# A hybrid decoder layer on one core: the values of the linear-attention branch stored as one array, and full copies moved behind both high halves

## The chip, the core and the metric

The kernel runs on one core of one Trainium2 chip. What counts is the device time of one execution in microseconds, as a median of several runs. Beside the times there is a profile of one execution. In it PE is TensorE's matmuls, PEld its weight loads, DVE VectorE, ACT ScalarE, POOL GpSimd, and SP the engine that here issues the DMAs (SPq in the rows is SP's queue of them).

## The reference

Input x has 1024 tokens of width 1024, all in float32. The layer normalizes x, projects it once with the wide matrix w_in, and feeds two token mixers: a gated linear attention (GLA, 4 heads, keys of 128, values of 256, a decay for each key channel) and a stick-breaking attention (8 heads of 128). Cut to what matters here:

```python
h = rmsnorm(x, norm_g)
proj = h @ w_in
(g_q, g_k, g_v, g_gate, g_rank,
 s_q, s_k, s_v, s_gate, m_logits) = jnp.split(proj, SPLIT_IDX, axis=-1)
log_a = jax.nn.log_sigmoid((g_rank @ w_dec_up + b_dec).astype(jnp.float32)) / GLA_TAU
o_gla = gla_chunked(g_q, g_k, g_v, log_a)      # o_t = q_t S_t, S_t = diag(alpha_t) S_{t-1} + k_t v_t
o_gla = rmsnorm(o_gla, gla_norm_g) * jax.nn.silu(g_gate)
o_sb = stick_breaking(s_q, s_k, s_v) * jax.nn.silu(s_gate)
gates = jax.nn.sigmoid(m_logits + b_gate)
merged = gates[:, :, 0] * (o_gla @ w_pa) + gates[:, :, 1] * (o_sb @ w_pb)
out = rmsnorm(x + merged @ w_o, final_g)
```

The change lies in the first tenth of this: h and its transposes, g_v (1024 columns, 256 for each head), and the handover to the decay logits (g_rank times w_dec_up).

## The kernel before

Every float32 operand of a matmul is split into a high half (ACT rounds it to the matmul type) and a low half (DVE subtracts the high half from it); `split` at L159 to L161 does both. Each product is then three matmuls: high by high, high by low, low by high.

**Arrival.** Eight tiles of 128 tokens come in one by one. For each one ACT sums the squares and DVE multiplies by the norm factors (xs, `norm_a` and `norm_b`); PE transposes it in two groups g of four 128x128 blocks, each group into one PSUM bank (`turn_x`, tag tr, two banks); the bank is split into a quarter of h (ha11, ha12, ha21, ha22, each with h for high and l for low); and ACT writes a full copy of the bank besides (`whole`, L403), since sums of quarters are needed later. The values of head 0 and the 16 columns of the decay code are projected by `first_v` at once (L218, 24 matmuls a tile; PE's order is a scheduler's, so these lie between the transposes). ACT and DVE work in the order in which the code is written here (`manual_schedule`), SP, PE and POOL in that of a scheduler. `VW_AT` puts the first three splits of value weights (`vq_split`) behind tiles 4, 5 and 6. At the end SP saves the quarter A21, both halves, 1 MB each (d_a), and loads the weight block B22.

**The value stage.** The values of heads 1 to 3 (768 columns) are one matrix product done in the Strassen-Winograd form: seven products of quarters u = 0 to 6 instead of eight, with sums S1 to S4 of h and T1 to T4 of the weights. Each is cut in two halves of the inner dimension and four token tiles t: 56 items of six matmuls, with k = 8u + 4jp + t. The list `due` says which work of ACT and DVE is issued behind item k, with `at(k, ...)`; PE, ACT and DVE follow the written order here. `v_evict` empties the banks: the results of tokens n and column half J go out through `v_put`, which stores each head's part into that head's own array, d_gv[h], so two DMAs for each 384 columns:

```python
for h, c0, o0, w in (((1, 0, 0, DV), (2, 0, DV, P)) if J == 0 else ((2, P, 0, P), (3, 0, P, DV))):
    nc.sync.dma_start(d_gv[h][:, tb, c0:c0 + w], c[:, o0:o0 + w])
```

Product u = 5 is collected in c, a tile with two buffers of one token tile each (tags dh and dl); u = 6 adds into the kept tiles s5 and p7 (named s and p in the rows) and stores from these.

**The decay code.** The space of the value stage is then given to pool dq: `wup` (w_dec_up) is loaded, split into `wst`, the transposed code into `rst` (`code`, L761), and `logit` multiplies them (L773). This runs beside the projections in pairs of column blocks (`Pairs`, also seven products u = 0 to 6 for each pair, twelve matmuls each, L265 to L267; L271 keeps a bank in f, L304 adds one up). `djobs` holds a list of decay work for each product of the pairs; the work stands ahead of that product's own. Later t_load and its like are spread in the same way, then the GLA blocks load their values with `gl_load` (tile vr) two blocks ahead, and the rest of the layer follows.

Of the kernel before, what the change touches and what calls it, by code (L numbers as in the profile page):

```python
# [15 lines left out]
P = 128  # L16
# [82 lines left out]
def hybrid_layer(ctx: ExitStack, tc: tile.TileContext, x, norm_g, w_in, w_up, b_dec,  # L99
# [25 lines left out]
    d_sg = dram_set("sg", SB_H, [P, T])  # L125
    d_osb = dram_set("osb", SB_H, [P, T])
    d_gq, d_gk, d_e1, d_e2 = (dram_set(nm, GLA_H, [P, T]) for nm in ("gq", "gk", "e1", "e2"))
    d_gv = dram_set("gv", GLA_H, [P, NT, DV])
    d_gg = dram_set("gg", GLA_H, [P, 2, T])
    d_ogl = dram_set("ogl", 2, [P, 2, GLA_H, T])  # L130
    d_ga, d_gb, d_ma = (dram_set(nm, KB, [P, T]) for nm in ("ga", "gb", "ma"))
# [249 lines left out]
        nc.vector.tensor_sub(dst, vq[x1], vq[x2_])  # L381
        vq[nm] = dst

    VW_AT = {4: (0, 0), 5: (0, 1), 6: (1, 0)}
    wh = {}

    def four(i, nm):
# [17 lines left out]
    with tc.tile_pool(name="p0", bufs=3, reuse_waits="tile") as p0:  # L405
# [47 lines left out]
        def first_v(tb):  # L453
            pt = proj_n(rows_of(ws0), hq, tb, VR, early=tb == 0)
            st = v_stage(tb)
            nc.vector.tensor_copy(st[:, tb % 2], pt[:, 0:DV])
            if tb % 2:
                nc.sync.dma_start(d_gv[0][:, tb - 1:tb + 1], st)
            nc.vector.tensor_copy(rcode[:, tb], pt[:, DV:VR])

        def turn_x(tb, gs=(0, 1)):
            xs = by_parity(xss[tb])
            for g in gs:
                pt = ps.tile([P, HALF], F32, tag="tr", name="tr")
                for j in range(4):
                    nc.tensor.transpose(pt[:, j * P:(j + 1) * P], xs[:, g, j], ident)
                cs = slice(tb % 4 * P, (tb % 4 + 1) * P)
                q = hq[tb // 4, g]
                split(pt.rearrange("p (a b) -> p a b", a=4), q[0][:, :, cs], q[1][:, :, cs])
                whole(tb, g, pt.rearrange("p (a b) -> p a b", a=4))  # L470

        with tc.manual_schedule(engines={mybir.EngineType.Activation, mybir.EngineType.DVE}):
            norm_a(0)
            (raw0, hi0, lo0), (raw1, hi1, lo1) = ws0
            norm_b(0, 0)
            norm_b(0, 1)
            xs = by_parity(xss[0])
            pts = []
            for g in range(2):
                pt = ps.tile([P, HALF], F32, tag="tr", name="tr")  # L480
                for j in range(4):
                    nc.tensor.transpose(pt[:, j * P:(j + 1) * P], xs[:, g, j], ident)
                pts.append(pt.rearrange("p (a b) -> p a b", a=4))
                nc.scalar.activation(hq[0, g][0][:, :, 0:P], pts[g], AF.Copy)
            nc.vector.tensor_copy(hi0, raw0)
            keep_warm(WARM[1])
            for g in range(2):
                nc.vector.tensor_sub(hq[0, g][1][:, :, 0:P], pts[g], hq[0, g][0][:, :, 0:P].bitcast(F32))
            norm_a(1)
            nc.vector.tensor_sub(lo0, raw0, hi0.bitcast(F32))  # L490
            nc.scalar.activation(hi1, raw1, AF.Copy)
            for g in range(2):
                whole(0, g, pts[g])
            norm_b(1, 0)
            nc.vector.tensor_sub(lo1, raw1, hi1.bitcast(F32))
            norm_b(1, 1)
            ws0 = [w[1:] for w in ws0]
            for tb in range(1, NT):
                if tb + 1 < NT:
                    norm_a(tb + 1)  # L500
                turn_x(tb)
                if tb + 1 < NT:
                    norm_b(tb + 1)
                first_v(tb - 1)
                if tb in VW_AT:
                    vq_split(*VW_AT[tb])
            first_v(NT - 1)
        load_cols(p0.tile([22, P], F32, tag="vrow", name="vrow", bufs=1))

# [140 lines left out]

    def v_put(n, J, t, c):

        tb = 4 * n + t
        for h, c0, o0, w in (((1, 0, 0, DV), (2, 0, DV, P)) if J == 0 else ((2, P, 0, P), (3, 0, P, DV))):
            nc.sync.dma_start(d_gv[h][:, tb, c0:c0 + w], c[:, o0:o0 + w])

    vx = [ps.tile([P, HALF], F32, tag=tag, name="vx")[:, 0:VH] for tag in ("z", "z", "tr", "tr")]
    vy, keep4 = {}, {}
# [18 lines left out]
    def v_evict(u, t):  # L677
# [5 lines left out]
        elif u in (2, 3):  # L683
            nm = ("p7", "s5")[u - 2]
            if t == 0:
                keep4[nm] = vq_tile(nm)
            nc.scalar.activation(keep4[nm][:, t], vy[t], AF.Copy)
        elif u == 5:
            c = sw.tile([P, 4, P], F32, tag="d" + "hl"[t % 2], name="c", bufs=1).rearrange("p a c -> p (a c)")[:, 0:VH]
            nc.scalar.activation(c, vy[t], AF.Copy)  # L690
            nc.vector.tensor_add(c, vx[t], c)
            v_put(0, 1, t, c)
        elif u == 6:
            for J, nm in ((1, "s5"), (0, "p7")):
                c = keep4[nm][:, t]
                nc.vector.tensor_add(c, vx[t], c)
                v_put(1, J, t, c)

    due = {k: [] for k in range(60)}
# [3 lines left out]

    for k, nm in ((0, "T1"), (1, "T2"), (6, "T4"), (17, "T3")):
        at(k, vq_sum, nm)
    for k, u, jp in ((5, 1, 1), (9, 2, 0), (13, 2, 1), (18, 3, 0), (21, 3, 1), (25, 4, 0), (28, 4, 1), (33, 5, 0), (37, 5, 1),
                     (41, 6, 0), (45, 6, 1)):
        at(k, vq_split, u, jp)
    for nm, ks, ls in (("S1", (3, 3, 4, 8), (10, 10, 15, 16)), ("S2", (19, 19, 20, 21), (23, 23, 24, 26)),
# [88 lines left out]
        nc.sync.dma_start(d_e1[h], E[h])  # L798
        nc.sync.dma_start(d_e2[h], U[h])

    djobs = [[(code, 0)], [(code, 1)]]
    for h in (0, 2):
        djobs += [[(logit, h)], [(logit, h + 1), (decay_a, h)], [(decay_b, h), (decay_a, h + 1)], [(decay_b, h + 1)],
                  [(decay_c, h), (decay_c, h + 1)], [(decay_d, h)], [(decay_e, h), (decay_d, h + 1)],
# [90 lines left out]
    def gl_load(h, b):  # L895

        v = gv.tile([P, DV], F32, tag="vr", name="vr", bufs=3)
        nc.sync.dma_start(v, d_gv[h][:, b])
        g = gv.tile([P, 2, P], F32, tag="g", name="g", bufs=3)
        nc.sync.dma_start(g, d_gg[h][:, :, b * P:(b + 1) * P])  # L900
        gblk[h, b] = {"vr": v, "g": g}
# [683 lines left out]
```

## Time and profile before

| | us |
|---|---|
| median of 3 runs | 1202.97 |
| lowest and highest | 1201.97, 1202.97 |
| the profiled execution | 1203.79 |
| its span | 1202.1 |
| PE busy | 1170.7 (97%) |
| DVE busy | 863.1 (72%) |
| ACT busy | 553.0 (46%) |
| POOL busy | 248.6 (21%) |

The profiled execution's time is 1.7 above its span, which runs from the first to the last instruction. A row of the timeline has start, duration, engine, line, operation, out<-in, partitions by elements and count, and in brackets the idle time before it with what ended it. A row of the chain has start, duration and who. A row of a stretch has its limits, its length, the busy time of PE, PEld, DVE, ACT and POOL with counts, the granted PE clock, the DMA share and GB/s. A row of waits has who waited for whom, the sum, the number of times and the longest.

### The profile page before, as it was taken

How to read it: one execution, taken by the hardware profiler on the slowest of the kernel's cores; microseconds unless marked ns; L12 is line 12 of the kernel's file. 1: busy time of each engine (PE TensorE's matmuls, PEld its weight loads, DVE VectorE, ACT ScalarE, POOL GpSimd, SP SyncE). 2: the span in 40 equal slices, each digit the busy share in tenths (PEclk: the TensorE clock that was granted, in tenths of full speed). 3: DMA queues.
4: the chain of work that ended last, by engine and by line, in shares of the span. 5: the costliest groups of instructions: out<-in, count | busy, mean ns of one | idle time of the engine just before them, and what ended most of it. 6: DMA issues, size and time to landing. Idle time of an engine off the chain costs nothing.

```text
span 1202.1 us, 16630 instructions
## 1 busy us (share of the span) xinstructions
PE 1170.7 (97%) x5811; PEld 981.5 (82%) x5811; DVE 863.1 (72%) x1440; ACT 553.0 (46%) x1040; POOL 248.6 (21%) x217
## 2 busy tenths in 40 slices
PE   8998899999999999999999999999999999999997
PEld 7897678888888888888888887888888888888886
DVE  5695586778677777777765667547687776488986
ACT  5552564342455445444534443324454544365543
POOL 1020252324432422423323322100000000700001
PEclk9998899999999999999999999999999999999999
DMA  7323257998545656655345346898867556848652
GB/s 282 124 62 94 88 188 264 359 305 292 172 133 182 216 184 184 210 166 175 129 142 158 121 140 199 241 341 311 270 201 234 174 169 194 298 152 278 230 193 105
DMA packets 191247, 239.23 MB, mean 199 GB/s; under 512 B 12694, under 2 KB 129452, under 8 KB 189628
## 3 DMA queue, kind: packets, MB, share of 16 engines
q1 hardware_dynamic: 190588, 237.13, 59.9%
q8 instruction: 45, 0.74, 0.3%
q10 hardware_dynamic: 576, 1.05, 0.2%
q14 instruction: 38, 0.31, 0.1%
HBM read 150.06 MB, written 88.08 MB: 198 GB/s over the span
## 4 chain that ended last, share of the span: by engine, by line
PE 85%; DVE 6%; DMA 4%; ACT 3%; issue 2%; SPq 0%; POOL 0%; ACTq 0%; DVEq 0%; POOLq 0%
PE pp L265 16%; PE pp L266 15%; PE pp L267 15%; PE pp L199 3%; PE pp L201 3%; PE pp L200 3%; PE av L1103 1%; PE av L1102 1%; PE av L1101 1%; PE tr L1080 1%; PE z L1062 1%; PE xb L1469 1%; PE xb L1468 1%; PE xb L1467 1%; PE z L1064 1%
## 5 line engine op out<-in xcount | busy, mean ns | idle before, releaser
L265 PE MATMUL pp<-S,wh 128*128 128x512 f32 x372 | 148.0, 398 | 0.0
L267 PE MATMUL pp<-S,wl 128*128 128x512 f32 x372 | 145.7, 392 | 0.0
L266 PE MATMUL pp<-S,wh 128*128 128x512 f32 x372 | 145.7, 392 | 0.0
L304 DVE TENSOR_TENSOR f<-pp,f 128x512 f32<-128x512 f32 x93 | 63.9, 688 | 68.0 <-PE pp L267 63.9
L161 DVE TENSOR_TENSOR wl<-tt,wh 128x1024 fp32r<-128x1024 f32 x62 | 76.7, 1237 | 47.1 <-ACT wh L160 46.6
L239 POOL TENSOR_TENSOR tt<-raw 128x512 f32<-128x512 f32 x31 | 44.5, 1435 | 261.6 <-DVE wl L161 240.6
L160 ACT ACTIVATE wh<-tt 128x1024 fp32r<-128x1024 f32 x62 | 65.6, 1059 | 71.6 <-PE pp L266 63.2
L271 ACT ACTIVATE f<-pp 128x512 f32<-128x512 f32 x93 | 54.9, 591 | 86.8 <-PE pp L267 83.5
L1068 DVE TENSOR_TENSOR_SCAN be<-be,m 128x128 f32<-128x128 f32 (+3 forms) x64 | 86.2, 1349 | 7.1 <-ACT be L1065 6.9
L160 ACT ACTIVATE wh<-raw 128x1024 fp32r<-128x1024 f32 (+1 forms) x47 | 48.4, 1030 | 82.8 <-PE pp L266 49.8
L265 PEld LDWEIGHTS pp<-S,wh 128*128 128x128 f32 x372 | 71.1, 191 | 15.0 <-ACT f L271 0.7
L267 PEld LDWEIGHTS pp<-S,wl 128*128 128x128 f32 x372 | 70.3, 189 | 15.0
L266 PEld LDWEIGHTS pp<-S,wh 128*128 128x128 f32 x372 | 70.4, 189 | 13.8
L161 DVE TENSOR_TENSOR wl<-raw,wh 128x1024 fp32r<-128x1024 f32 (+1 forms) x47 | 65.5, 1394 | 18.2 <-ACT wh L160 17.5
L226 POOL TENSOR_TENSOR r<-r,nhalf 128x1 f32<-128x1 f32 x40 | 26.6, 664 | 200.9 <-DVE r L225 200.9
L1252 POOL TENSOR_TENSOR N<-A,A 128x512 f32<-128x512 f32 x4 | 6.6, 1654 | 243.1 <-DVE bB21l L1294 243.1
L1065 ACT ACTIVATE be<-z 128x384 f32<-128x384 f32 (+4 forms) x96 | 46.9, 494 | 20.9 <-PE z L1064 18.4
L265 PE MATMUL pp<-S,dh 128*128 128x512 f32 x124 | 48.7, 393 | 0.6 <-ACT f L271 0.6
L265 PE MATMUL pp<-ha11h,wh 128*128 128x512 f32 x124 | 49.1, 396 | 0.0
L265 PE MATMUL pp<-ha12h,wh 128*128 128x512 f32 x124 | 49.1, 396 | 0.0
L265 PE MATMUL pp<-ha22h,wh 128*128 128x512 f32 x124 | 48.8, 394 | 0.2 <-DVE f L304 0.2
L242 POOL TENSOR_TENSOR tt<-raw,tt 128x512 f32<-128x512 f32 x31 | 48.3, 1557 | 2.3
(528 smaller groups left out, 3401.1 us busy)
## 6 DMA issues: line engine op xcount, KB each, us to landing
raw<-in_w_in_dram SPq DMA_DIRECT2D x31, 1024.0 KB, 6.3
d_t<-t SPq DMA_DIRECT2D x16, 512.0 KB, 5.1
d_ogl<-o SPq DMA_DIRECT2D x64, 128.0 KB, 2.6
d_q<-o SPq DMA_DIRECT2D x16, 512.0 KB, 4.2
d_k<-o SPq DMA_DIRECT2D x16, 512.0 KB, 4.8
d_v<-o SPq DMA_DIRECT2D x32, 256.0 KB, 2.6
k<-d_k SPq DMA_DIRECT2D x8, 1024.0 KB, 7.1
v<-d_v SPq DMA_DIRECT2D x16, 512.0 KB, 5.7
```

The source lines that it names most:

```text
L160: nc.scalar.activation(hi, src, AF.Copy)
L161: eng.tensor_sub(lo, src, hi.bitcast(F32))
L199: nc.tensor.matmul(pt, whi[:, kb], h_, start=kb == 0, stop=False)
L239: nc.gpsimd.tensor_sub(t1, b[:, 0, 1], b[:, 0, 0])
L242: nc.gpsimd.tensor_sub(t4, b[:, 1, 0], t2)
L265: nc.tensor.matmul(pt, bh[:, j], ah[:, j], start=first and j == 0, stop=False, skip_group_check=True)
L266: nc.tensor.matmul(pt, bh[:, j], al[:, j], start=False, stop=False, skip_group_check=True)
L267: nc.tensor.matmul(pt, bl[:, j], ah[:, j], start=False, stop=j == 3, skip_group_check=True)
L271: nc.scalar.activation(t[nm], t[bank], AF.Copy)
L304: nc.vector.tensor_add(add, bank, add)
L1065: nc.scalar.activation(om[:, off + pc * w:off + (pc + 1) * w], zt[:, 0:w], AF.Sigmoid, scale=-inv_sqrt)
L1068: nc.vector.tensor_tensor_scan(rest, rest, m1[:, off:T][:, ::-1], 1.0, op0=ALU.mult, op1=ALU.max)
```

## The change

The values of all four heads go to one array d_gv of 128 by 8 by 1024, so a `v_put` is one DMA of 384 columns, and `gl_load` reads a head's 256 columns out of it. In u = 5 the tile c is replaced by a stage buffer that holds two token tiles; in u = 6 the sums go to a stage buffer (J = 0) and to tiles f (J = 1) instead of back into p7 and s5. In `turn_x` the splits of both groups come first, then both full copies. The value splits of arrival stand behind the last tile, the third of them in the value stage at item 1. And `djobs` begins with an empty list, so that all decay work comes one product later.

```diff
-    d_gv = dram_set("gv", GLA_H, [P, NT, DV])
+    d_gv = dram.tile([P, NT, GLA_H * DV], F32, tag="gv", name="d_gv")
...
-    VW_AT = {4: (0, 0), 5: (0, 1), 6: (1, 0)}
+    VW_AT = {7: ((0, 0), (0, 1))}
...
-                nc.sync.dma_start(d_gv[0][:, tb - 1:tb + 1], st)
+                nc.sync.dma_start(d_gv[:, tb - 1:tb + 1, 0:DV], st)
...
             xs = by_parity(xss[tb])
+            pts = []
             for g in gs:
...
-                split(pt.rearrange("p (a b) -> p a b", a=4), q[0][:, :, cs], q[1][:, :, cs])
-                whole(tb, g, pt.rearrange("p (a b) -> p a b", a=4))
+                pt = pt.rearrange("p (a b) -> p a b", a=4)
+                split(pt, q[0][:, :, cs], q[1][:, :, cs])
+                pts.append(pt)
+            for g, pt in zip(gs, pts):
+                whole(tb, g, pt)
...
-                if tb in VW_AT:
-                    vq_split(*VW_AT[tb])
+                for u, jp in VW_AT.get(tb, ()):
+                    vq_split(u, jp)
...
-        tb = 4 * n + t
-        for h, c0, o0, w in (((1, 0, 0, DV), (2, 0, DV, P)) if J == 0 else ((2, P, 0, P), (3, 0, P, DV))):
-            nc.sync.dma_start(d_gv[h][:, tb, c0:c0 + w], c[:, o0:o0 + w])
+        nc.sync.dma_start(d_gv[:, 4 * n + t, DV + J * VH:DV + (J + 1) * VH], c)
...
         elif u == 5:
-            c = sw.tile([P, 4, P], F32, tag="d" + "hl"[t % 2], name="c", bufs=1).rearrange("p a c -> p (a c)")[:, 0:VH]
+            if t % 2 == 0:
+                keep4["c"] = stage().bitcast(F32)
+            c = keep4["c"][:, t % 2, 0:VH]
             nc.scalar.activation(c, vy[t], AF.Copy)
             nc.vector.tensor_add(c, vx[t], c)
             v_put(0, 1, t, c)
         elif u == 6:
-            for J, nm in ((1, "s5"), (0, "p7")):
-                c = keep4[nm][:, t]
-                nc.vector.tensor_add(c, vx[t], c)
+            if t % 2 == 0:
+                keep4["c"] = stage().bitcast(F32)
+            for J, c in ((1, ev.tile([P, HALF], F32, tag="f", name="f")[:, 0:VH]), (0, keep4["c"][:, t % 2, 0:VH])):
+                nc.vector.tensor_add(c, vx[t], keep4[("p7", "s5")[J]][:, t])
                 v_put(1, J, t, c)
...
-    for k, u, jp in ((5, 1, 1), (9, 2, 0), (13, 2, 1), (18, 3, 0), (21, 3, 1), (25, 4, 0), (28, 4, 1), (33, 5, 0), (37, 5, 1),
+    for k, u, jp in ((1, 1, 0), (5, 1, 1), (9, 2, 0), (13, 2, 1), (18, 3, 0), (21, 3, 1), (25, 4, 0), (28, 4, 1), (33, 5, 0), (37, 5, 1),
...
-    djobs = [[(code, 0)], [(code, 1)]]
+    djobs = [[], [(code, 0)], [(code, 1)]]
...
-        nc.sync.dma_start(v, d_gv[h][:, b])
+        nc.sync.dma_start(v, d_gv[:, b, h * DV:(h + 1) * DV])
```

How this moves instructions, at three places. First ACT in arrival, tiles 4 and 5 (xs is the sum of squares, ha21h and ha22h are the high halves, w and o the full copies of the two groups, wh a value split); before:

```order
L433 ACTIVATE xs,ssq<-xt 128x1024
L160 ACTIVATE ha21h<-tr 128x4x128
L403 ACTIVATE w<-tr 128x512
L160 ACTIVATE ha22h<-tr 128x4x128
L403 ACTIVATE o<-tr 128x512
L160 ACTIVATE wh<-vq 128x768
```

And now:

```order
L433 ACTIVATE xs,ssq<-xt 128x1024
L160 ACTIVATE ha21h<-tr 128x4x128
L160 ACTIVATE ha22h<-tr 128x4x128
L403 ACTIVATE w<-tr 128x512
L403 ACTIVATE o<-tr 128x512
```

The second high half has moved ahead of the first full copy, and the value split has left the round.

Second, SP's DMAs at the end of arrival (vst are the values of head 0, d_a the saves of A21, B the weight block B22); before:

```order
L458 DMA d_gv_132<-vst 128x512 x3
L520 DMA d_a_166<-ha21h 128x2048
L368 DMA B_707<-in_w_in_dram 128x4x384
L520 DMA d_a_167<-ha21l 128x2048
L458 DMA d_gv_132<-vst 128x512
```

And now:

```order
L458 DMA d_gv<-vst 128x2x256 x2
L524 DMA d_a_163<-ha21h 128x2048
L524 DMA d_a_164<-ha21l 128x2048
L368 DMA B_700<-in_w_in_dram 128x4x384
L458 DMA d_gv<-vst 128x2x256
```

The load of B22 has moved from between the two saves to behind both.

Third, the end of the value stage and the start of the decay code. SP there, with the last token tile's stores, the next weight load (raw) and wup; before:

```order
L655 DMA d_gv_134<-s_995 128x128
L655 DMA d_gv_135<-s_995 128x256
L655 DMA d_gv_133<-p_912 128x256
L655 DMA d_gv_134<-p_912 128x128
L235 DMA raw<-in_w_in_dram 128x8x256
L744 DMA wup<-in_w_dec_up_dram 16x512
```

And now, from the last but one token tile's stores on:

```order
L657 DMA d_gv<-f 128x384
L657 DMA d_gv<-o 128x384
L235 DMA raw<-in_w_in_dram 128x8x256
L657 DMA d_gv<-f 128x384
L657 DMA d_gv<-o 128x384
L749 DMA wup<-in_w_dec_up_dram 16x512
```

A token tile has two stores where it had four, and the weight load stands one token tile earlier. ACT at the same place, from the next pair's first splits (wh, dh) to the first product's keep (f, L271); before:

```order
L160 ACTIVATE dh<-raw 128x512
L757 ACTIVATE wst<-wup 16x512 x2
L757 ACTIVATE rst<-tr 16x512 x2
L160 ACTIVATE wh<-tt 128x1024
L271 ACTIVATE f<-pp 128x512
L757 ACTIVATE rst<-tr 16x512 x2
L160 ACTIVATE wh<-raw 128x1024
```

And now:

```order
L160 ACTIVATE dh<-raw 128x512
L160 ACTIVATE wh<-tt 128x1024
L271 ACTIVATE f<-pp 128x512
L762 ACTIVATE wst<-wup 16x512 x2
L762 ACTIVATE rst<-tr 16x512 x4
L160 ACTIVATE wh<-raw 128x1024
```

The keep and the last split of the first pair have moved ahead of the decay matrix, and all four rst copies ahead of the next pair's split. In PE's order the first two logits (L773 before, L778 now) stand behind three products of the pairs before and behind four now; the next pair's first two matmuls come right behind them, and then the fifth product.

## The prediction

> **What bounds the kernel now.** I read the page's busy shares first, then PE's waits, then the chain of waits, the timeline and the stretches around the places that they name.
>
> ```profile
> PE 1170.7 (97%) x5811; PEld 981.5 (82%) x5811; DVE 863.1 (72%) x1440; ACT 553.0 (46%) x1040; POOL 248.6 (21%) x217
> PE vx L673 <- DVE c L691: 5.8, 1, 5.8
> PE tr L773 <- DVE rst L759: 5.7, 1, 5.7
> PE pp L218 <- ACT ha12h L160: 1.9, 3, 0.7
> 290.00:670.00 380.00, 380.00 (x1870) 1.00 0.54 172
> ```
>
> PE is the bound: 1202.1 - 1170.7 = 31.4 us is all that it stands idle, and from 290 to 670 us it does not stop. The waits at the top of its list (us in total, times, longest) all lie before 135 us, where the change is: two single ones of 5.8 and 5.7, and short ones in arrival. What PE gets back there nothing later can hide, since PE is full behind it.
>
> **Arrival.** One round is a closed chain; here the third tile's, from its transposes on, with the starts of three rounds below it:
>
> ```profile
> 24.79 0.61 ACT ha11h L160
> 25.41 0.70 DVE ha11l L161
> 26.14 0.60 ACT w L403
> 26.74 0.50 ACT ha12h L160
> 27.26 0.70 DVE ha12l L161
> 27.87 1.27 DVE L443 SCALAR_TENSOR_TENSOR xs<-xt,r,gb 128x1024 f32<-128x1024 f32 x1
> 18.93 1.04 PE L466 MATMUL tr<-ident,xs 128*128 128x128 f32 x8
> 24.15 1.04 PE L466 MATMUL tr<-ident,xs 128*128 128x128 f32 x8
> 46.75 1.04 PE L466 MATMUL tr<-ident,xs 128*128 128x128 f32 x8
> 24.94 0.50 PE L218 MATMUL pp<-vw,ha12h 128*128 128x272 f32 x2
> 26.41 0.29 PE L218 MATMUL pp<-vw,ha11l 128*128 128x272 f32 x1
> 40.14 0.95 DVE L161 TENSOR_TENSOR wl<-vq,wh 128x768 fp32r<-128x768 f32 x1
> ```
>
> The full copy (w, L403) starts only when DVE has left its bank (25.41 + 0.70 = 26.11, start 26.14), and the second high half stands behind it on ACT. From one set of transposes to the next it is 5.22 us (18.93 to 24.15). With both high halves first, the first one comes 0.64 after the transposes, as now, and its low half at 1.26, as now. The second high half starts about 0.5 behind the first, so the second low half follows the first directly, 0.61 later (27.26 to 27.87 is what one low half takes before the next work): 1.87. Then the gain (xs) at 2.48, lasting 1.27, and the next transposes 0.22 behind it: 3.97. PE's own work in a round is 0.79 for the transposes (24.15 to 24.94) and 23 matmuls at 0.134 (11 of them from 24.94 to 26.41), 3.87: it just fits under. The second full copy now ends 1.87 + 0.70 + 0.04 + 0.60 = 3.2 after the transposes, and its bank is wanted again at 3.97; that is the slack that hides both copies.
>
> Five rounds lie between the transposes at 18.93 and those at 46.75 (27.8 us). The last two are longer than 5.2 because two value splits (0.95 on DVE each) and a 1.76 sum stand in them; these go behind arrival. So 5 x 3.97 = 19.9, and the last transposes come at 38.8, 7.9 earlier. The first round, whose second transposes are late for another reason, I leave as it is. But 16 of the 48 matmuls of the first value product run in arrival's gaps now and cannot any more. From the last transposes on PE has 0.8 + 38 x 0.134 + 8 items of 1.04 = 14.2 us to the second product, which until now began at 58.94, 12.2 behind them. It starts at 53.0: **5.9 us gained**.
>
> What is late next: the load of B22 now stands behind both saves of A21 instead of between them.
>
> ```profile
> 48.01 0.32 SPq L520 DMA_DIRECT2D d_a<-ha21h  x1
> 48.90 0.99 SPq L520 DMA_DIRECT2D d_a<-ha21l  x1
> d_a<-ha21l SPq DMA_DIRECT2D x1, 1024.0 KB, 9.0
> 55.53 1.76 DVE L381 TENSOR_TENSOR T<-B,vq 128x1536 f32<-128x1536 f32 x1 [1.46 <-DMA B<-in_w_in_dram]
> 58.94 0.33 PE L673 MATMUL pp<-wh,ha12h 128*128 128x384 f32 x1
> ```
>
> The three together took from 48.0 to 57.9, and B22 landed at 55.5. Now the first save can go at 40.1 (the last tile's high half: 38.8 + 0.64 + 0.61), so that B22, last of the three, lands by about 50.0 to 50.9. DVE then takes T2 (1.76) and behind it the low half of the second product's first split (0.95), which was done inside arrival before: 52.7 to 53.6, and PE wants it at 53.0. I take 0.3 us of stall, between 0 and 3 (landing 9.0 after its own issue near 42, the worst of the rows, and one more DVE sum before it).
>
> **The value stage.** From 58.94 to 103.65 PE ran 43 items, 1.04 each, without a gap. Then:
>
> ```profile
> 103.48 0.34 PE L675 MATMUL vx<-wh,S 128*128 128x384 f32 x1
> 99.86 0.38 SPq L235 DMA_DIRECT2D raw<-in_w_in_dram  x1
> 100.92 7.46 DMA d_gv<-c
> 109.62 0.69 PE L673 MATMUL vx<-wh,S 128*128 128x384 f32 x1 [5.80 <-DVE c L691]
> 116.51 0.39 PE L265 MATMUL pp<-ha11h,wh 128*128 128x512 f32 x1
> ```
>
> Tile c has two buffers for four token tiles: the fourth copy waits until the second one's store has landed, and that store was issued just behind a 1 MB weight load. PE stood, and came back at a lower clock. The five items left took 103.65 to 116.51, 12.9 us. With c in two-tile stage buffers no copy of the sixth product waits for a store; five items at 1.04 take 5.2: **7.7 gained**. The stage ends at 53.0 + 0.3 + 48 x 1.04 = 103.2. The seventh product's third result does reuse the buffer of those stores, at about 102.5; the weight load moves 5.9 earlier, to 94.0, and the store lands 8.5 after it as now, at 102.5. If it is late, DVE waits, and no PE work stands behind that.
>
> **The decay code.** Now the way goes through SP:
>
> ```profile
> 114.18 0.80 SPq L655 DMA_DIRECT2D d_gv<-s  x2
> 118.59 0.55 DVE L696 TENSOR_TENSOR p<-vx,p 128x384 f32<-128x384 f32 x1
> 122.73 0.41 SPq L235 DMA_DIRECT2D raw<-in_w_in_dram  x1
> 123.19 4.95 DMA wup<-in_w_dec_up_dram
> 128.23 1.28 ACT L757 ACTIVATE wst<-wup 16x512 fp32r<-16x512 f32 x2 [14.62 <-DMA wup<-in_w_dec_up_dram]
> 129.52 1.18 ACT L757 ACTIVATE rst<-tr 16x512 fp32r<-16x512 f32 x2
> 116.50:125.70 9.20, 9.20 (x45) 7.14 (x44) 2.64 (x6) 0.00 (x0) 1.98 (x3) 1.00 0.60 181
> 131.53 0.80 PE L773 MATMUL tr<-rst,wst 128*128 128x512 f32 x1 [5.71 <-DVE rst L759]
> 131.50:137.00 5.50, 5.47 (x12) 3.78 (x13) 4.83 (x6) 2.88 (x5) 3.80 (x4) 0.50 0.12 48
> 141.33 0.39 PE L265 MATMUL pp<-S,dh 128*128 128x512 f32 x1
> ```
>
> Sixteen stores start at 114.18, 0.4 each, and end 3.5 behind DVE's last sum (119.1, itself 2.6 behind PE's end); then a weight load, then the small decay matrix wup, landing 11.6 us behind the stage's end. Now eight stores are issued as fast as DVE delivers. DVE ends at 103.2 + 2.6 = 105.8, two stores follow, and wup goes at 106.7. With the 5.0 of now it lands at 111.7; counted from the weight load's issue, a sum and a store earlier (104.8, and 5.4 as now), at 110.2. Logits came 3.4 behind the landing (128.1 to 131.5): 113.6 to 115.1. PE has two reasons not to wait by then: the empty first job puts one whole product more ahead of the logits, and ACT takes the first product's keep before the decay matrix instead of after it. Three products and both transposes took 9.15, a product 2.8; four bring PE to 115.2. Right behind the first logit stands the next pair's first split on ACT, which now follows two wst and four rst copies: 0.1 + 1.28 + 2 x 1.18 + 1.06 = 4.8 behind the landing, 115.0 to 116.5. I take 0.5 us of wait, between 0 and 1.0. From the stage's end to the mark at 141.33 it took 24.8 us. The work there (five products, 0.7 for transposes, 0.9 for four logits, 0.5 for two matmuls of the next pair) is 16.2, with the wait 16.7: **8.1 gained**, some 5.7 of it idle time and 2.7 the clock of 0.50.
>
> The stores' longer rows and the loads of values from a wider row I take at nothing: the stores have no PE work waiting any more, and the loads run two blocks ahead (rows below). In the rest of the decay chain, one product later on PE's side, I take no change.
>
> **Sum.** 5.9 - 0.3 + 7.7 + 8.1 = 21.4. The profiled execution took 1203.79 (span 1202.1 and 1.7 around it): 1182.4. It lay 0.8 above the median of 1202.97: 1181.6. I say **1182 us**, 1179 to 1186 if things go this way; 1178 would take 25 of the 31.4 us that PE idles in the whole program.
>
> **Rivals.** *The decay matrix stays late* (0.10). For it: it is still issued last, behind a 1 MB load, and the margin at the logits is 0.1 to 1.6. Against: PE has 2.8 us more work ahead and SP eight stores fewer. If wup lands at 115.5, PE waits 3.7 at 115.2, and if the clock falls, 2.7 more: 1188.
>
> ```profile
> 106.00:107.00 1.00, 0.00 (x0) 0.00 (x0) 0.00 (x0) 0.00 (x0) 0.00 (x0) 0.63 0.28 82
> ```
>
> Here the clock fell (mean 0.63) already some 2.6 us after PE stopped at 103.65, so a wait of 3.7 pays for it. [...]
>
> *Arrival's gain is eaten* (0.10). If B22 lands 3 us later, the second product stalls, since DVE serves its list in a written order; or rounds take 4.8, because PE at 3.87 queues behind the copies' banks. Then 3 to 5 of the 5.9 are lost: 1187.
>
> *Slower* (0.02): the loads of values from the joined array, whose rows lie four times as far apart.
>
> ```profile
> L898 SPq DMA_DIRECT2D vr<-d_gv x32: 319/552/1034, 296.9 to 665.4; - x32
> DMA to landing us min/median/max: 2.4/3.0/7.0
> ```
>
> They come every 11.9 us, two ahead: 23.8 us of cover over 3.0. What lies above that counts up to 32 times; at 24.5 us a load the gain is gone and at 25 the kernel is 17 us slower than before. The longest is 7.0, so it gets next to nothing. [...]
>
> **Chances.** As forecast 0.75, the decay rival 0.10, arrival 0.10, slower 0.02, and 0.03 that new waits cancel the gains. The range of 1178 to 1190 holds the forecast and both smaller gains. A change of 0.2%, 2.4 us, is about what can be told from none: faster 0.95, within 0.03, slower 0.02.
>
> **What would show it.** Transposes every 4.0 us in arrival; the second product at 53; no PE wait on the sixth product's sums and no clock of 0.50 after the start; the value stage ending near 103; wup landing at 110 to 112; the mark of 141.3 near 120. It is wrong if T2 waits for B22 past 51, if the logits still hold PE over 2 us, or if PE loses behind 190 us what it won before.

## The result: faster by about 10 us, not by 21

The changed kernel takes 1193.94 us (median of 4 runs), the kernel before 1202.97. One of the four, at 1655 us, had a granted PE clock of 0.65 from 10 us to its end; the ratio is that of the other three (median 1193.55), 0.992, with a 95% interval of 0.990 to 0.994. I had said 1182, 1178 to 1190. The direction is right and the size is wrong by half. The profile after is that of a second set of runs of the same kernel, e_again below: median 1190.9 (1189.67 to 1194.24), ratio 0.990 [0.9875, 0.993], span 1189.8, 12.3 below the 1202.1 of before. Why the second set is some 3 us faster than the first stays open.

First the page's busy shares of the changed kernel and the head of PE's list of waits (who waits for whom, us in total, times, longest), then the places that the prediction named:

```profile
PE 1165.0 (98%) x5811; PEld 978.8 (82%) x5811; DVE 859.5 (72%) x1440; ACT 553.3 (47%) x1040; POOL 247.1 (21%) x217
PE pp L265 <- DVE f L304: 5.8, 1, 5.8
PE pp L265 <- ACT f L271: 1.8, 2, 1.1
...
PE pp L265 <- ACT wh L160: 1.0, 1, 1.0
```

```profile
34.31 1.06 PE L467 MATMUL tr<-ident,xs 128*128 128x128 f32 x8
38.23 1.06 PE L467 MATMUL tr<-ident,xs 128*128 128x128 f32 x8
...
52.62 0.33 PE L675 MATMUL pp<-wh,ha12h 128*128 128x384 f32 x1
...
111.46 1.29 ACT L762 ACTIVATE wst<-wup 16x512 fp32r<-16x512 f32 x2 [5.35 <-DMA wup<-in_w_dec_up_dram]
...
114.77 0.49 PE L778 MATMUL tr<-rst,wst 128*128 128x512 f32 x1 [0.23 <-DVE rst L764]
...
116.29 0.50 PE L265 MATMUL pp<-ha11h,wh 128*128 128x512 f32 x1 [1.02 <-ACT wh L160]
...
120.29 0.39 PE L265 MATMUL pp<-S,dh 128*128 128x512 f32 x1
...
132.05 0.50 PE L265 MATMUL pp<-S,wh 128*128 128x512 f32 x1 [1.13 <-ACT f L271]
149.95 0.79 PE L265 MATMUL pp<-ha22h,wh 128*128 128x512 f32 x1 [5.79 <-DVE f L304]
```

Both waits of 5.8 and 5.7 that stood at the top before are gone, and a single new one of 5.8 us has taken their place, at 150 us. At the mark (the row at 120.29, which was at 141.33) the kernel is 21.0 us ahead. After that it loses. A second mark shows it: the first matmul of the GLA blocks (`pa`, in `gl_local`), behind all decay work. Its row gives the first and last start; first the changed kernel's, then that of before:

```profile
L915 PE MATMUL pa<-q,ke x64: 272/298/324, 300.2 to 689.1; 128*64 128x128 f32 x64
```

```profile
L910 PE MATMUL pa<-q,ke x64: 272/298/324, 313.0 to 702.0; 128*64 128x128 f32 x64
```

300.2 against 313.0 is 12.8: of the 21.0 us, 8.2 are gone by then. From there to the end of the span the two differ little (889.6 and 889.1 us).

**Where the 8.2 us went.** Between the mark and 200 us PE waits 1.13 at 132, 5.79 at 150, and the other 0.7 of the second row of the list above; the kernel before waited 1.4 there (0.6, 0.6 and 0.2). That is 6.2 more. The rest is clock. In stretches of the changed kernel around 150 (limits, length, busy time of PE, PEld, DVE, ACT, POOL, granted clock, DMA):

```profile
146.00:148.00 2.00, 0.00 (x0) 0.00 (x0) 0.00 (x0) 1.97 (x4) 0.00 (x0) 0.94 0.60 248
...
150.00:152.00 2.00, 2.00 (x5) 1.61 (x6) 2.00 (x4) 0.00 (x0) 0.00 (x0) 0.50 0.62 242
...
154.00:156.00 2.00, 2.00 (x9) 1.65 (x8) 0.62 (x1) 0.86 (x2) 0.00 (x0) 0.85 0.99 320
```

PE works again from 149.95 and has its full clock near 154.6: some 4.6 us at half speed, 2.3 lost. 6.2 and 2.3 make 8.5, for the 8.2 that are missing.

**What holds PE at 150.** The matmul at 149.95 adds into a bank that the total of L304 must have read. Here are ACT, DVE and POOL of the changed kernel from 134 us on:

```profile
137.25 1.06 ACT L798 ACTIVATE e<-u 128x1024 f32<-128x1024 f32 x1 [0.22 <-DVE u L795]
138.34 1.06 ACT L799 ACTIVATE u<-u 128x1024 f32<-128x1024 f32 x1
139.31 0.58 ACT L271 ACTIVATE f<-pp 128x512 f32<-128x512 f32 x1
144.95 1.06 ACT L798 ACTIVATE e<-u 128x1024 f32<-128x1024 f32 x1 [5.06 <-DVE u L795]
146.03 1.06 ACT L799 ACTIVATE u<-u 128x1024 f32<-128x1024 f32 x1
147.00 1.04 ACT L160 ACTIVATE wh<-tt 128x1024 fp32r<-128x1024 f32 x1
```

```profile
137.14 2.25 DVE L792 SCALAR_TENSOR_TENSOR e<-u,e 128x1024 f32<-128x1024 f32 x1
139.31 2.31 DVE L161 TENSOR_TENSOR wl<-raw,wh 128x1024 fp32r<-128x1024 f32 x1
141.54 3.37 DVE L795 TENSOR_TENSOR_SCAN u<-rmask,e 128x1024 f32<-128x1024 f32 x1
...
148.07 1.23 DVE L161 TENSOR_TENSOR wl<-tt,wh 128x1024 fp32r<-128x1024 f32 x1 [3.09 <-ACT wh L160]
149.21 0.68 DVE L304 TENSOR_TENSOR f<-pp,f 128x512 f32<-128x512 f32 x1
```

```profile
138.26 2.27 POOL L240 TENSOR_TENSOR tt<-raw,tt 128x512 f32<-128x512 f32 x1
140.61 2.15 POOL L242 TENSOR_TENSOR tt<-raw,tt 128x512 f32<-128x512 f32 x1
```

Read it backwards. The total (149.21) stands behind a low half (148.07), which waits for its high half on ACT (147.00). The data of that high half, two quarters of tt, are complete when POOL's L240 ends at 140.53, but ACT serves its list in order, and ahead of it stand the two exponentials of the second head (144.95, 146.03), which wait for that head's scan on DVE (141.54). The same stretch of the kernel before, on ACT:

```profile
158.40 1.06 ACT L793 ACTIVATE e<-u 128x1024 f32<-128x1024 f32 x1 [1.90 <-DVE u L790]
159.50 1.06 ACT L794 ACTIVATE u<-u 128x1024 f32<-128x1024 f32 x1
160.46 0.58 ACT L271 ACTIVATE f<-pp 128x512 f32<-128x512 f32 x1
160.94 1.05 ACT L160 ACTIVATE wh<-tt 128x1024 fp32r<-128x1024 f32 x1
```

There the exponentials stand one product earlier, ahead of the keep of L271, and the split starts 0.4 us behind them. The decay lists are tied to positions in the pairs' products, and the pairs put the splits for the next pair at u = 2, 4 and 6 only (the last one at that pair's own u = 0). One product later for all decay work is therefore not a delay of equal size for everything: the exponentials came to stand directly ahead of the split at u = 4, and the second scan behind the low half at u = 2 instead of ahead of it.

### The profile page after: what moved, and what is told of

Same layout as the page of the kernel before. It is cut to its first block, busy times and chain, and to the rows that moved or that the text cites. A ratio compares the mean times of both kernels' runs of the same rounds, so it can differ in the third digit from the quotient of the medians.

```text
span 1653.3 us, 16605 instructions
## 1 busy us (share of the span) xinstructions
PE 1643.2 (99%) x5811; PEld 1121.4 (68%) x5811; DVE 845.0 (51%) x1440; ACT 564.9 (34%) x1040; POOL 237.8 (14%) x217
## 4 chain that ended last, share of the span: by engine, by line
PE 99%; DMA 0%; ACT 0%; SPq 0%; DVE 0%; issue 0%; ACTq 0%
PE pp L267 17%; PE pp L265 17%; PE pp L266 17%; PE pp L200 3%; PE pp L201 3%; PE pp L199 3%; PE pp L218 2%; PE tr L1085 2%; PE av L1107 2%; PE av L1108 2%; PE av L1106 1%; PE z L1068 1%; PE z L1067 1%; PE z L1069 1%; PE xb L1474 1%; PE pp L1085 1%
## 5 line engine op out<-in xcount | busy, mean ns | idle before, releaser
L265 PE MATMUL pp<-S,wh 128*128 128x512 f32 x372 | 190.8, 513 | 0.0
L267 PE MATMUL pp<-S,wl 128*128 128x512 f32 x372 | 188.6, 507 | 0.0
L266 PE MATMUL pp<-S,wh 128*128 128x512 f32 x372 | 188.3, 506 | 0.0
L304 DVE TENSOR_TENSOR f<-pp,f 128x512 f32<-128x512 f32 x93 | 64.3, 691 | 200.1 <-PE pp L267 187.9
L271 ACT ACTIVATE f<-pp 128x512 f32<-128x512 f32 x93 | 55.2, 593 | 184.1 <-PE pp L267 175.0
L267 PEld LDWEIGHTS pp<-S,wl 128*128 128x128 f32 x372 | 77.1, 207 | 43.3 <-issue 13.8
L266 PEld LDWEIGHTS pp<-S,wh 128*128 128x128 f32 x372 | 78.2, 210 | 41.6 <-issue 14.0
L265 PEld LDWEIGHTS pp<-S,wh 128*128 128x128 f32 x372 | 76.9, 207 | 42.4 <-issue 15.2
L265 PE MATMUL pp<-ha12h,wh 128*128 128x512 f32 x124 | 63.8, 514 | 0.0
L265 PE MATMUL pp<-ha11h,wh 128*128 128x512 f32 x124 | 63.5, 512 | 0.0
L265 PE MATMUL pp<-S,dh 128*128 128x512 f32 x124 | 63.5, 512 | 0.0
L265 PE MATMUL pp<-ha22h,wh 128*128 128x512 f32 x124 | 63.3, 511 | 0.1
L267 PE MATMUL pp<-ha12h,wl 128*128 128x512 f32 x124 | 63.0, 508 | 0.0
L267 PE MATMUL pp<-ha11h,wl 128*128 128x512 f32 x124 | 62.9, 507 | 0.0
```

The lines of the kernel that those rows point to most:

```text
L265: nc.tensor.matmul(pt, bh[:, j], ah[:, j], start=first and j == 0, stop=False, skip_group_check=True)
L266: nc.tensor.matmul(pt, bh[:, j], al[:, j], start=False, stop=False, skip_group_check=True)
L267: nc.tensor.matmul(pt, bl[:, j], ah[:, j], start=False, stop=j == 3, skip_group_check=True)
L271: nc.scalar.activation(t[nm], t[bank], AF.Copy)
L304: nc.vector.tensor_add(add, bank, add)
```

## The experiments

All are compared with the kernel before on the same chip; its median lies between 1202.71 and 1203.77 in these comparisons, so medians of different runs compare with each other to about 1 us. The last column is the first start of `pa`; the kernel before has 313.0 in the profile shown.

| run | what | median us | ratio, 95% interval | `pa` at |
|---|---|---|---|---|
| e_again | the whole change | 1190.9 | 0.990 [0.9875, 0.993] | 300.2 |
| e_arrival | arrival alone | 1196.43 | 0.9945 [0.9926, 0.9964] | 306.3 |
| e_stores | stores and buffers alone | 1193.37 | 0.992 [0.9901, 0.9939] | 303.3 |
| e_nodecay | whole, no empty list | 1187.34 | 0.9868 [0.9852, 0.9885] | 296.7 |
| e_shift | empty list alone | 1210.78 | 1.0068 [1.0053, 1.0083] | 318.0 |
| e_merge | whole, only the logits late | 1183.5 | 0.9838 [0.9822, 0.9855] | 293.2 |
| e_wup | no empty list, early matrix | 1180.05 | 0.9806 [0.9791, 0.9821] | 289.3 |
| e_full_wup | whole, early matrix | 1190.58 | 0.9902 [0.9884, 0.992] | 298.2 |
| e_fmove | whole, exponentials behind the split | 1187.93 | 0.9875 [0.9856, 0.9893] | 296.9 |
| e_fe_move | and the scan one list later | 1186.67 | 0.9869 [0.9854, 0.9884] | 295.6 |
| e_fe_behind | and the scan behind the total | 1188.0 | 0.988 [0.9862, 0.9898] | 294.5 |
| e_stage | two-tile buffers for c alone | 1196.51 | 0.995 [0.9933, 0.9967] | 306.7 |
| e_wup_only | early matrix alone | 1196.86 | 0.9953 [0.9936, 0.9971] | 306.4 |

### The parts one by one

e_again is the changed kernel itself.

> The changed kernel again, for a trace of an execution at full clock. My steps: second value product at 53, value stage ending at 103, mark near 120, 1182 us. Rival (arrival's gain is eaten): transposes further apart than 4.0 us or T2 late, value stage ending at 107 to 109. Rival (decay matrix late): value stage at 103, but a PE wait of 3 to 6 us at the logits with a clock of 0.50 behind it. The first times of 1192 to 1194 say that some 12 us of the 21.4 were not gained: the trace is to show at which of the three places, or behind them.

e_arrival is the kernel before with the new order in `turn_x` and the moved value splits only (the third split goes to item 1, as in the change):

```diff
-    VW_AT = {4: (0, 0), 5: (0, 1), 6: (1, 0)}
+    VW_AT = {7: ((0, 0), (0, 1))}
...
-                split(pt.rearrange("p (a b) -> p a b", a=4), q[0][:, :, cs], q[1][:, :, cs])
-                whole(tb, g, pt.rearrange("p (a b) -> p a b", a=4))
+                pt = pt.rearrange("p (a b) -> p a b", a=4)
+                split(pt, q[0][:, :, cs], q[1][:, :, cs])
+                pts.append(pt)
+            for g, pt in zip(gs, pts):
+                whole(tb, g, pt)
```

> The kernel before with arrival's part alone: both high halves first, then the copies, and the value splits behind the last tile; stores and decay code as before. My steps: 5.9 less, 1197. Rival (arrival's gain is eaten): 1202 to 1203, no gain. Rival (what the weight load triggers): the first wait on tile c grows as the stage starts earlier, 1198 to 1200.

It gained 6.3 us (1202.71 to 1196.43).

e_stores is the kernel before with the one array, its stores and loads, and the buffers of u = 5 and u = 6; arrival and decay code as before.

> The kernel before with one array, one store a block and the wider buffers alone; arrival and the start of the decay work as before. My steps: 7.7 from the sixth product's wait and 3 to 6 at the logits, 1189 to 1192. Rival (arrival eaten, so that the stores carry all that the change gives): the same time as the whole change, 1192 to 1194. Rival (decay late): 7.7 alone, 1195.

It gained 9.3 us. The wait at the logits fell with it, from 5.7 to 2.9, since the decay matrix goes out earlier behind half as many stores.

e_nodecay is the whole change without its last part:

```diff
-    djobs = [[], [(code, 0)], [(code, 1)]]
+    djobs = [[(code, 0)], [(code, 1)]]
```

> The whole change without the empty first job, so that the decay work keeps its place among the products. My steps: one product (2.8 us) less of cover at the logits, so 2 to 5 us slower than the whole change. Rival (decay matrix lands early enough anyway): the same time. Rival (the shift itself costs behind 150 us): 1 to 3 us faster than the whole change.

It is 3.6 us faster than the whole change. Its gain of 15.4 is nearly that of the other two parts together (6.3 + 9.3 = 15.6; at `pa` 16.3 against 6.7 + 9.7). So these two add up and keep what they gain, and the empty list takes away from it.

### The shift alone

```diff
-    djobs = [[(code, 0)], [(code, 1)]]
+    djobs = [[], [(code, 0)], [(code, 1)]]
```

> The kernel before with one edit: the empty first list ahead of the decay code. Theory (the shift makes its own wait): with every decay job one product later, ACT has the exponentials of the second head ahead of the next pair's split and DVE's total waits behind that split, so PE stands about 6 us near 170 and loses the clock as it does near 150 in the whole change; what the cover at the logits saves (the 5.7 us wait shrinks to about 3 and part of the clock's 2.7 us) is lost again: 1200 to 1205, same as before. Rival (the wait near 150 needs the other two parts, and the shift alone is pure cover, as my prediction took it): 5 to 8 us faster, about 1196.

On the kernel before the empty list costs 7.0 us, more than either theory said: 5.0 of them at `pa` (318.0 against 313.0), the rest behind it. PE's list of waits of this run:

```profile
PE pp L265 <- DVE f L304: 5.8, 1, 5.8
...
PE tr L773 <- DVE rst L759: 2.7, 1, 2.7
```

The wait near 150 is there again, at 168.49 here and of the same 5.8, so it needs neither of the other parts. The saving at the logits is smaller than I put it: the wait falls from 5.7 to 2.7, but a new 0.73 stands behind it, and the clock falls all the same. PE stopped at 128.5 and is at half clock from 130.49 to 137.32 (rows in the last section), so the clock's whole cost stays: 6.8 us at 0.50, as in the kernel before (130.15 to 136.98). The rival, that the shift is pure cover as the prediction took it, falls.

What is lost behind `pa` is not in this run alone. From the first start of `pa` to the end of the span the six kernels with the whole decay chain one product later (e_again, e_shift, e_full_wup, e_fmove, e_fe_move, e_fe_behind) take 889.6 to 890.9 us, and the eight others 887.7 to 889.1. In the stick-breaking part PE waits once for ACT's half afh: 1.1 to 2.0 us in those six, 0.7 or less in the others. So the shift seems to have a small price there too, 1.8 us on the average; by what way, no run shows.

### The logits late, the rest not

The whole change, with the empty list, but both logits of heads 0 and 1 in one list. So the logits keep the cover that the change gives them, and every later decay job goes back to its old product:

```diff
-        djobs += [[(logit, h)], [(logit, h + 1), (decay_a, h)], [(decay_b, h), (decay_a, h + 1)], [(decay_b, h + 1)],
+        djobs += [[(logit, h)]] if h else []
+        djobs += [[(logit, h + 1), (decay_a, h)] if h else [(logit, 0), (logit, 1), (decay_a, 0)], [(decay_b, h), (decay_a, h + 1)], [(decay_b, h + 1)],
```

> The whole change, with the empty first list kept, but both logits of the first two heads in one list, so that the two logits stay where the change put them and all later decay jobs go one product back, to where they were before. Theory: the wait of 2.9 us at the logits stays away as in the whole change, the wait of 5.8 us near 150 is gone as it is without the empty list: 1187.3 - 2.9 - 1 to 2 of clock = 1183 to 1185. Rival (the hole comes from the logits being late, not from where the later jobs stand): no gain over 1190.9.

1183.5, 7.4 below the whole change. Neither the 2.9 us wait of e_nodecay nor the 5.8 is left, and the clock is 1.00 from 105 to 200. The longer waits that remain in that stretch are two for ACT's keeps of L271 (0.57 at 137.36 and 1.51 at 141.89) and 1.02 for the split of the next pair.

### The matrix early instead of the logits late

The change without the empty list, and wup loaded behind item 41 of the value stage into a tile f that is free there:

```diff
+    def wup_load():
+        keep4["wup"] = ev.tile([P, HALF], F32, tag="f", name="f")[0:RANK]
+        nc.sync.dma_start(keep4["wup"], w_up)
+    at(41, wup_load)
...
-    wup = dq.tile([RANK, GLA_H * P], F32, tag="wup", name="wup")
-    nc.sync.dma_start(wup, w_up)
+    wup = keep4["wup"]
```

> The change without the empty first list (1187.3), and with the small decay matrix loaded about 13 us earlier, into a tile that is free in the last products of the value stage. Theory: the 2.9 us wait at the logits, which came from the matrix landing 111 behind the last stores and a 1 MB weight load, goes to 0.5 or less with the 0.9 to 2 us of clock that it cost, and nothing stands in its place: 1183 to 1185. Rival (the split of the next pair on ACT and POOL is late by as much anyway): 1186 to 1187.

1180.05, 7.3 below e_nodecay where I expected 3 to 4. The load goes out at 83.47, 22.4 us earlier than in e_nodecay (105.90), and not some 13 as I had put it. The high halves of wst are made at 100.05 now, before the value stage ends, and the first logit stands at 109.14 with no wait. PE in the same stretch, first e_nodecay, then e_wup:

```profile
105.00:125.00 20.00, 16.91 (x67) 12.80 (x67) 10.35 (x13) 8.48 (x13) 7.69 (x7) 0.91 0.30 90
125.00:160.00 35.00, 32.92 (x142) 26.03 (x142) 26.42 (x25) 24.04 (x28) 14.71 (x8) 1.00 0.51 180
```

```profile
105.00:125.00 20.00, 20.00 (x91) 16.33 (x90) 14.60 (x18) 13.49 (x18) 5.88 (x6) 1.00 0.35 114
125.00:160.00 35.00, 34.45 (x151) 27.90 (x151) 29.51 (x26) 23.33 (x27) 15.95 (x8) 1.00 0.47 166
```

3.1 us of waits and 0.09 x 20 = 1.8 of clock come back in the first stretch, as the theory had it, and 1.5 more of waits in the second, which it had not: the waits of 0.55 and 1.07 for ACT's keeps that e_nodecay has at 140.49 and 145.03 are gone. That earlier logits give the whole decay chain slack is the likely reason. This kernel beats both: from 60 to 300 us it waits less than 1 us.

The same early load on the whole change, empty list included, and on the kernel before:

> The whole change with its empty first list, and the small decay matrix loaded 13 us earlier, so that the list has nothing left to cover. Theory (the shift by itself costs what stands at 132 and 150 in the whole change: 1.1 + 5.8 us of waits and about 2.3 of clock): 1180.1 + 8 to 9 = 1187 to 1190, so that the early load is worth some 7 us without the list and 1 to 3 with it. Rival (the later jobs only ran late because the matrix and so the logits were late): 1180 to 1183.

> The kernel before with only the small decay matrix loaded some 13 us before the end of the value stage. Theory: of the 5.7 us at the logits all goes, with 2.7 us of clock, and no wait takes its place since the later jobs keep their products: 8.4 gained, 1194 to 1196; that is more than the whole change's 8.1 at this place, for one load. Rival (the copies behind the matrix are late for another reason, DVE's last sums and PE's transposes): 2 to 4 gained, 1199 to 1201.

With the empty list the early matrix gains little: 2.0 us at `pa`, and nothing that can be told in the medians (1190.58 against 1190.9). The wait for the total of L304 is still there, at 146.95 and 6.2 us long now.

Between e_wup and e_full_wup the empty list is the only difference, with nothing left to cover: 8.9 us at `pa` (289.3 to 298.2), 10.5 in the medians. That is the shift's own price.

Alone on the kernel before, the early matrix gained 6.3 where I expected 8.4. The wait at the logits is gone with its clock, 5.7 + 2.7 as expected, and the wait on c is 0.9 shorter (4.9). Against that stand 1.0 more of waits for ACT's keeps (L271: 1.6, where the kernel before had 0.6) and 1.7 lost in arrival, which this edit does not touch: there the clock of the profiled execution fell at 45.68 (last section), and the second product starts at 60.60 instead of 58.94. Together that is the 6.6 by which it is ahead at `pa`.

### What the wait at 150 is made of

Three kernels move the second head's jobs in the whole change. First its exponentials alone, one list later and so behind the split:

```diff
-                  [(decay_f, h), (decay_e, h + 1)], [(decay_f, h + 1), (decay_g, h)], [(decay_g, h + 1)]]
+                  [(decay_f, h), (decay_e, h + 1)], [(decay_g, h)], [(decay_f, h + 1), (decay_g, h + 1)]]
```

> The whole change, with the second head's two exponentials one product later, so that the next pair's split stands ahead of them on ACT; nothing else moves. Theory (ACT's written order makes the wait: the split's high half waited from 142.8, when POOL had its data, to 147.0 behind the exponentials, which wait for DVE's scan): the high half comes up to 4 us earlier, the total on DVE about 3 us earlier (it still has the scan ahead of it), the wait falls from 5.8 to about 3 or less and the clock is kept: about 5 us less than the whole change, 1185 to 1187. Rival (the scans on DVE, drawn out beside POOL's subtractions, are the bound): 1190 to 1191 as before the edit.

The wait falls by 2.7 and the kernel by 3.0, not by 5: behind the 3.07 that are left the clock fell once more, to 0.50 at 145.5 (the first matmul behind the wait takes 0.79).

```profile
140.38 1.06 ACT L160 ACTIVATE wh<-tt 128x1024 fp32r<-128x1024 f32 x1 [0.68 <-POOL tt L240]
141.35 3.37 DVE L795 TENSOR_TENSOR_SCAN u<-rmask,e 128x1024 f32<-128x1024 f32 x1
144.71 1.22 DVE L161 TENSOR_TENSOR wl<-tt,wh 128x1024 fp32r<-128x1024 f32 x1
146.58 0.79 PE L265 MATMUL pp<-ha22h,wh 128*128 128x512 f32 x1 [3.07 <-DVE f L304]
```

The high half is ready at 141.4 now, but its low half comes only at 144.7, behind the scan. So I moved the scan too, one list later (`[(decay_f, h)], [(decay_e, h + 1), (decay_g, h)]`):

> The run with the second head's exponentials one product later (1187.9, wait 3.07), and now that head's scan one product later as well, so that on DVE too the split's low half and the total stand ahead of it. Theory (two engines' written orders make the wait, ACT's first, DVE's next: the high half was ready at 141.4, DVE was in the scan from 141.35 to 144.7): low half at 141.4, total at 142.6, before PE gets there at 143.5; the wait goes to 0.5 or less and with it the clock's 2 us: 1182 to 1184. Rival (DVE and ACT have too little time in this stretch in any order, so the delay only moves behind the next head's logits): 1186 to 1189.

The wait stayed at 3.07. The list of a product stands ahead of that product's split, so one list later the scan was still ahead of the low half on DVE (its rows are those of the run above, 0.04 us later): the edit did not do what I meant, and says nothing on the theory. That it is 1.3 us ahead of that run at `pa` is the clock's doing: half clock lasted 3.4 us here and 6.8 there, behind the same wait. One list more puts it behind:

```diff
-        djobs += [[(logit, h)], [(logit, h + 1), (decay_a, h)], [(decay_b, h), (decay_a, h + 1)], [(decay_b, h + 1)],
+        djobs += [[(logit, h)], [(logit, h + 1), (decay_a, h)] + ([(decay_g, h - 1)] if h else []),
+                  [(decay_b, h), (decay_a, h + 1)], [(decay_b, h + 1)],
...
-                  [(decay_f, h), (decay_e, h + 1)], [(decay_f, h + 1), (decay_g, h)], [(decay_g, h + 1)]]
+                  [(decay_f, h)], [(decay_g, h)], [(decay_e, h + 1), (decay_f, h + 1)]]
+    djobs += [[(decay_g, 3)]]
```

(decay_g of h + 1 goes two lists on, into the work of the next two heads.)

> The whole change, with the second head's scan and exponentials two lists later than there, so that on ACT and on DVE the split of the next pair and the total stand ahead of them (in the run with the scan one list later the scan still stood ahead of the split in DVE's order, as its rows show, and the wait stayed at 3.07). Theory: the high half comes at 140.4 when POOL has its data, the low half at about 141.5, the total at 142.7, PE gets there at 143.5: the wait goes to 0.5 or less, the clock is kept: 1182 to 1184. Rival (too little time on DVE in any order): the wait moves to the next pair's low halves or the third head's logits, 1186 to 1189.

```profile
143.76 0.68 DVE L304 TENSOR_TENSOR f<-pp,f 128x512 f32<-128x512 f32 x1
144.36 2.27 DVE L795 TENSOR_TENSOR_SCAN u<-rmask,e 128x1024 f32<-128x1024 f32 x1
144.49 0.50 PE L265 MATMUL pp<-ha22h,wh 128*128 128x512 f32 x1 [0.89 <-DVE f L304]
```

The wait falls to 0.89 and the clock stays at 1.00, as the theory says: 5.8 us are 2.7 for the exponentials, 2.2 for the scan, and 0.9 that is left. The time did not follow all the way. At `pa` the kernel is 5.7 ahead of the whole change and 1.1 ahead of the run before it, but waits of 0.6 for DVE's u and 1.6 for ACT's keeps (0.7 in the whole change) stand behind it up to 300 us, and the median of 1188.0 (1186.62 to 1189.41) lies between the rival's bounds. So both hold: the two written orders made the wait, and part of a job put later is waited for later. Putting jobs still later is the worse cure; e_merge, which puts them back, waits 0.2 us from 160 to 300.

### The buffers alone

The kernel before with c in two-tile stage buffers, and nothing else of the change:

```diff
-            c = sw.tile([P, 4, P], F32, tag="d" + "hl"[t % 2], name="c", bufs=1).rearrange("p a c -> p (a c)")[:, 0:VH]
+            if t % 2 == 0:
+                keep4["c"] = stage().bitcast(F32)
+            c = keep4["c"][:, t % 2, 0:VH]
```

> The kernel before with only the sixth product's tile c in two-tile stage buffers; two arrays' stores, arrival and decay code as before. Theory (the buffer takes the 5.8 us wait and its 2 us of clock; the single stores are worth the rest of the 9.3 that stores and buffers gained together, by the decay matrix's earlier issue): 7.7 gained, 1194 to 1196, with the wait at the logits still 5 to 6. Rival (the one store per block does it all; sixteen stores still hold the stage buffers): 1200 to 1203.

6.6 gained of the 7.7 expected, and the wait at the logits stays, 5.5 where it was 5.7. In the profiled execution the clock fell once in arrival here too (at 45.42, last section), and the second product starts at 60.48 instead of 58.94; without these 1.5 us the 6.3 at `pa` would be 7.8. So the buffers take the wait on the stores. The one store for each block, with the other buffers of u = 6, is worth the rest of e_stores, 2.7 in the medians (3.4 at `pa`, of which 1.5 is arrival's clock). There the decay matrix goes out at 112.22 instead of 116.83, and the wait at the logits is 2.6 shorter.

## Why the prediction was wrong

Point by point, by its own steps:

- *Arrival*: rounds of 3.97 forecast, 3.92 measured (34.31 to 38.23). B22 landed at 48.85, before the earliest I allowed (50.0), and there was no stall. The second product starts at 52.62, forecast 53.0 and 0.3 of stall behind it. Alone it gained 6.3 for the 5.9. Right.
- *The value stage*: no wait on the sixth product, and the pairs' first matmul at 102.54, where the forecast had the stage end at 103.2. Right; the buffers alone measured 6.6 for my 7.7, and in their profile, but for arrival's clock, 7.8 at `pa`.
- *The decay code up to the mark*: wup ready for ACT at 111.46 (110.2 to 111.7), the logits at 114.77 with 0.23 of wait, the split of the next pair 1.02 late (0.5, at most 1.0), the mark at 120.29 (near 120). Right to half a microsecond: 21.0 us of gain at the mark for the sum's 21.4. That it is so close is in part luck, since the stage's end 0.7 early makes up for the split 0.5 later than put.
- *"In the rest of the decay chain, one product later on PE's side, I take no change."* This is the step that failed, and it cost 8.2 us. I costed the empty list as three products of cover becoming four and looked at what it moved only as far as the logits. It moved every later decay job too, each past or in front of a split, on two engines that serve a written order. The wait at 150 and its clock come from there, 5.8 + 2.3: e_shift has them without the rest of the change, e_nodecay and e_merge lack them with the rest of it. (The 1.1 at 132 is no such term: e_nodecay and e_merge wait 0.6 and 1.1 to 1.5 for ACT's keeps instead, at 137 to 145.) The prediction's sign for such a loss looked behind 190 us; the loss came at 132 to 155.
- *The rivals*: the decay matrix staying late and arrival's gain eaten did not occur. The loads of values from the joined array cost nothing that shows: 2.8 us (median) from issue to landing where it was 3.0, and no PE wait on them. None of my rivals was the one that came; the 0.03 for new waits had neither a place nor a price, though the row that would have priced it stood in the profile: before, ACT's split at 160.94 started 0.4 us behind the exponentials, so there was no room for a later scan.

The forecast's sum would have been nearly right for a kernel one edit away: e_merge has the change with its cover and without the late jobs, 1183.5.

## What to carry to other kernels

When work is spread over positions of another loop, an offset of one moves every job of the chain past that loop's own work: follow it on each engine to the last job, and write down what stands ahead of each split or total then. Cover for a late transfer is bought more cheaply at the transfer (16 rows of weights, loaded 22 us earlier: 7.3 us gained) than by moving its users (3.6 lost). Waits of 2 to 3 us had no fixed price in clock here: 2.04 cost none (e_fe_move), and 3.07 cost 1.5 in one run (e_fe_move) and 2.9 in another (e_fmove), so give such a wait a range. And when a wait goes, compare a second mark well behind the change before believing the first.

## What the runs showed of the hardware

**A wait of 2.73 us lost the clock, and one of 2.04 us lost none.** In the profiled executions of eleven of the kernels the granted clock fell to 0.50 seventeen times between 18 and 200 us. It stayed there some 3.4 us eight times and some 6.8 us nine times (6.83 twice in the kernel before, from 106.26 and from 130.15). Here are stretches of e_shift around the last two of its three falls, with limits laid 3.41 us apart (limits, length, busy time and count of PE, clock, DMA):

```profile
127.08:130.49 3.41, 1.40 (x7) 1.00 0.02 7
130.49:133.90 3.41, 1.96 (x4) 0.50 0.20 77
133.90:137.32 3.42, 3.42 (x10) 0.50 0.00 0
...
161.22:164.63 3.41, 1.48 (x7) 1.00 0.00 0
164.63:168.04 3.41, 0.00 (x0) 1.00 0.75 308
168.04:171.45 3.41, 2.96 (x7) 0.50 0.40 154
```

The wait of 2.73 lost the clock 2.0 us behind PE's stop, that of 5.79 only 5.3 behind it. In arrival the clock fell to 0.50 in two of these executions, at 45.68 in e_wup_only and at 45.42 in e_stage. Here is e_stage, where PE had stood 1.42 of the 3.41 us ahead of the fall:

```profile
42.01:45.42 3.41, 1.99 (x11) 1.25 (x9) 2.26 (x4) 1.10 (x3) 1.32 (x1) 1.00 0.01 2
45.42:48.84 3.42, 3.41 (x15) 3.41 (x16) 2.43 (x4) 1.32 (x2) 0.00 (x0) 0.50 0.20 77
```

This wait, in e_fe_move, left the clock at 1.00:

```profile
839.77 0.50 PE L1106 MATMUL av<-afh,v 128*128 128x512 f32 x1 [2.04 <-ACT afh L160]
```

Why the clock falls behind one wait and not behind another, and why it stays down 3.4 us or 6.8, is open.

**Four DVE instructions took 3.7 us longer beside POOL.** DVE's subtraction of 128x1024 took 1.22 with POOL idle (144.71 in e_fmove) and 2.31 at 139.31 in the changed kernel; its scan took 2.27 with POOL idle (144.36 in e_fe_behind) and 3.37 at 141.54. POOL's instructions of the time ended at 140.53 and 142.76, and DVE's 1.09 and 2.15 later. Beside POOL's four subtractions in the changed kernel (132.86 to 142.76) four instructions of the chain to PE took longer: the first head's scan (2.78), the second head's subtraction (2.25), a low half (2.31) and the second head's scan (3.37), 3.7 us more in all than they took elsewhere (2.27 and 1.22). By what way, no run shows, and what the chain would take without POOL's subtractions was not tried.
